# Linear attention: K and V read in 8 KB rows over eight heads, K's features kept twice, first matmul 128 wide

## Chip, cores and metric

The kernel runs on one core of a Trainium2 chip. The metric is device time in microseconds (us) of one execution. The core has these engines: PE (TensorE, matmuls; its weight loads are shown as PEld), DVE (VectorE), ACT (ScalarE), POOL (GpSimd) and SP (SyncE). DMAs are issued here by POOL and SP and run on 16 DMA engines that the queues share.

## The reference

```python
batch, heads, seq, dim = 8, 12, 512, 64          # Q, K, V: float32

Q_feat = np.maximum(0, Q) + 1
K_feat = np.maximum(0, K) + 1
KV = np.einsum('bhkd,bhkv->bhdv', K_feat, V)      # 64 x 64 per head
K_sum = np.sum(K_feat, axis=2)
numerator = np.einsum('bhqd,bhdv->bhqv', Q_feat, KV)
denominator = np.einsum('bhqd,bhd->bhq', Q_feat, K_sum)
return numerator / (denominator[:, :, :, None] + 1e-10)
```

There are 96 heads (batch times heads), each of 512 rows of 64 features. Three inputs of 12.58 MB are read and one output of 12.58 MB is written.

## The kernel before

**Tiling.** The 96 heads are handled as 12 groups of 8 heads, numbered 0 to 11, and the groups in 6 pairs (2s, 2s+1). The code calls the group `g` and the pair `s`. K and V are viewed with 16 sequence rows on a partition (`k_dram`, `v_dram`, C2 = 16), so one contiguous run in DRAM is 16 x 64 float32, 4 KB, and one 128-partition slab holds 4 heads, 32 partitions to a head. A group is two such slabs (index `n`, the slabs g and g + 2 of a pair's four). Q is viewed with 32 rows on a partition (`q_eights`), a run of 8 KB, 16 partitions to a head.

**Loads.** Except for the first K, which SP loads as float32 (`load_first_k`), all loads are issued by POOL and are turned from float32 into bf16 on the way. `load_pair(s)` issues K, V and Q of a pair, 2 MB each in DRAM and 1 MB in SBUF. `in_pool` has two buffers of each, so the loads of pair s + 2 are issued after the groups of pair s have used theirs; this stands at the end of an odd group's iteration.

**Per group.**
- `k_features(g)` (DVE, L137): kf = max(K + 1, 1), two instructions of 128 x 1024 elements.
- `v_blocks(g)`: V is copied into `v_all[:, g % 2]`, which is block-diagonal. Partitions 32b to 32b+31 (head b of a slab) have V in columns 64b to 64b+63, and ones in column 256 + b; the rest is zero. Three of the four copies are on DVE (L155), one is on ACT (L153).
- `keys_values(g)` (PE, L171): 32 matmuls with 64 columns of weights and a moving side of 260 columns. Slab n = 0 writes PSUM partitions 0 to 63, slab n = 1 writes 64 to 127. The two run side by side in two halves of the array. ACT then copies the result (`kva_ps`) into `kva_diag[g % 4]` in four instructions (L181, L182), again block-diagonal over n.
- `q_features`, `transposes` (PE L192 and ACT L195): the features of Q, transposed.
- `out_matmuls(g, h)` and `norms(g, h)` for h = 0, 1: 16 matmuls (L205) with `kva_diag` as the moving side, then a reciprocal (L222) and a product (L223) on DVE, twice. Here g is the pair member whose columns of Q are taken, and h chooses the K/V group: `kva_diag[(g // 2 * 2 + h) % 4]`. So h = 0 needs `keys_values` of the pair's even group and h = 1 that of its odd group.
- `store(g)`: 1 MB of output, by POOL for groups 0 to 9, by SP for 10 and (in two halves) 11.

**Order.** The order of instructions on every engine is the order written out in the code (`tc.manual_schedule()`). In the main loop (groups 0 to 9) an iteration of an odd group is: transposes(g-1), k_features(g), v_blocks(g), output(g-2), transposes(g), keys_values(g), loads and a store. An iteration of an even group is: k_features(g), v_blocks(g), output(g-2), q_features of g and g+1, keys_values(g), and a store. The last pair is written out by hand: k_features(10), output(8), out_matmuls(9, 0), v_blocks(10), k_features(11), v_blocks(11), keys_values(10), q_features of both, norms(9, 0), transposes(10), out_matmuls(9, 1), norms(9, 1), transposes(11), keys_values(11), output(10), output(11), stores. POOL's queue is in order too: a store that waits for its norms holds up the loads written behind it.

Of the kernel before, what the change touches and what calls it, by code (L numbers as in the profile page):

```python
# [8 lines left out]
FP32 = mybir.dt.float32  # L9
BF16 = mybir.dt.bfloat16  # L10
ALU = mybir.AluOpType
# [8 lines left out]
def kernel(  # L20
# [19 lines left out]
    nc = tc.nc  # L40

    B, H, S, D = Q.shape
    P = 128
    C = 8
    C2 = 2 * C
    C4 = 4 * C
    R = 4
    NPAIR = B * H * S // (P * C)
# [5 lines left out]
    def view(t, c):  # L54
        return t.flatten_outer_dims().rearrange("(n p c) d -> p n c d", p=P, c=c)

    q_eights = view(Q, C4)
    k_dram = view(K, C2)
    v_dram = view(V, C2)
    o_dram = view(out, C)  # L60

    const = ctx.enter_context(tc.tile_pool(name="const", bufs=1))
# [9 lines left out]
    psum_qt = ctx.enter_context(tc.tile_pool(name="psum_qt", bufs=2, space=bass.MemoryType.PSUM))  # L72

    identity = const.tile([P, P], BF16, name="identity")
    NV = 4
    v_all = const.tile([P, 2, 2, C2, 4 * D1], BF16, name="v_all")
    ones = const.tile([P, 4], BF16, name="ones")
    zero = const.tile([P, 1], FP32, name="zero")
    kva_all = const.tile([P, NV, 4, 2, D1], BF16, name="kva_all")
    kva_diag = [kva_all[:, i] for i in range(NV)]  # L80

    drams = dict(k=k_dram, v=v_dram)
    raw = {}
    bufs = {}
    kfs = {}
# [3 lines left out]
    cells_of = {}  # L89

    def load_first_k():
        k_raw = head_pool.tile([P, 2, C2, D], FP32, name="k_first")
        nc.sync.dma_start(out=k_raw, in_=k_dram[:, 0:4:2])
        raw["k", 0] = k_raw

    def load(x, groups):
        s = groups[0] // 2
        if groups[0] % 2 == 0 or (x, s) not in bufs:
            bufs[x, s] = in_pool.tile([P, 4, C2, D], BF16, name=f"{x}_raw")
        if len(groups) == 2:  # L100
            ms = slice(0, 4)
            of = slice(4 * s, 4 * s + 4)
        else:
            ms = slice(groups[0] % 2, 4, 2)
            of = slice(4 * s + groups[0] % 2, 4 * s + 4, 2)
        nc.gpsimd.dma_start(out=bufs[x, s][:, ms], in_=drams[x][:, of])  # L106
        for g in groups:
            raw[x, g] = bufs[x, s][:, g % 2 : 4 : 2]

    def load_q(s):  # L110
        t = in_pool.tile([P, 2, C4, D], BF16, name="q_raw")
# [28 lines left out]

    def k_features(g):
        k_raw = raw.pop(("k", g))
        kf = kf_pool.tile([P, C2, 2, D], BF16, name="kf")
        for n in range(2):
            feature(kf[:, :, n], k_raw[:, n])
        kfs[g] = kf

    def v_blocks(g):
        v_raw = raw.pop(("v", g))
        for b in range(4):  # L150
            ps = slice(32 * b, 32 * b + 32)
            if b == 3:
                nc.scalar.copy(out=v_all[ps, g % 2, :, :, b * D : b * D + D], in_=v_raw[ps])  # L153
            else:
                nc.vector.tensor_copy(  # L155
                    out=v_all[ps, g % 2, :, :, b * D : b * D + D], in_=v_raw[ps]
                )

    def q_features(g):
        q_raw = raw.pop(("q", g))  # L160
# [5 lines left out]
    def keys_values(g):  # L166
        kf = kfs.pop(g)
        kva_ps = psum_kva.tile([P, 4 * D1], FP32, name="kva_ps")
        for c in range(C2):
            for n in range(2):  # L170
                nc.tensor.matmul(  # L171
                    kva_ps[64 * n : 64 * n + 64],
                    lhsT=kf[:, c, n, :],
                    rhs=v_all[:, g % 2, n, c, :],
                    start=(c == 0),
                    stop=(c == C2 - 1),
                )
        kva = kva_diag[g % NV]
        for n in range(2):
            ps = slice(64 * n, 64 * n + 64)  # L180
            nc.scalar.copy(out=kva[ps, :, n, 0:D], in_=kva_ps[ps, 0 : 4 * D].rearrange("p (b d) -> p b d", b=4))  # L181
            nc.scalar.copy(out=kva[ps, :, n, D], in_=kva_ps[ps, 4 * D : 4 * D1])  # L182

    def transposes(g):
        qf = qfs.pop(g)
# [10 lines left out]

    def out_matmuls(g, h):
        qt = qts[g // 2]
        kva = kva_diag[(g // 2 * 2 + h) % NV]
        ops = [psum.tile([P, 2, BANK], FP32, tag="ps", name="o_ps") for _ in range(2)]  # L200
        for c in range(C):
            for j in range(2):
                b = 2 * (g % 2) + j
                q = 16 * (4 * h + b)
                nc.tensor.matmul(  # L205
                    ops[c // 4][64 * j : 64 * j + 64, c // 2 % 2, (c % 2) * W : (c % 2) * W + W],
                    lhsT=qt[:, c, q : q + 16, :],
                    rhs=kva[:, b],
                    start=True,
                    stop=True,  # L210
                )
        cells_of[g, h] = ops
# [19 lines left out]
    def output(g):  # L232
        for h in range(2):
            out_matmuls(g, h)
            norms(g, h)

    def clear(i):
        t = v_all[:, i].rearrange("p n c x -> p (n c x)").bitcast(FP32)
        w = t.shape[1] * 5 // 8
        nc.vector.memset(t[:, 0:w], 0.0)  # L240
        nc.scalar.copy(out=t[:, w:], in_=zero.to_broadcast([P, t.shape[1] - w]))  # L241
        nc.vector.tensor_copy(
            out=v_all[:, i, :, :, 4 * D : 4 * D1].rearrange("p n c j -> p (n c) j"),
            in_=ones[:, None, :].to_broadcast([P, 2 * C2, 4]),
        )

    with tc.manual_schedule():
        nc.gpsimd.memset(zero, 0.0)
        load_first_k()
        load("v", (0,))  # L250
        load_q(0)
        load("k", (1,))
        load("v", (1,))
        nc.vector.memset(ones, 0.0)
        for b in range(4):
            nc.vector.memset(ones[32 * b : 32 * b + 32, b : b + 1], 1.0)
        clear(0)
        make_identity(nc, identity)
        for t in kva_diag:
            for b in range(4):  # L260
                nc.gpsimd.memset(t[:, b], 0.0)  # L261
        load_pair(1)
        clear(1)
        last = NG - 1
        for g in range(last - 1):
            if g % 2:
                transposes(g - 1)
            k_features(g)
            v_blocks(g)
            if g >= 2:  # L270
                output(g - 2)
            if g % 2:
                transposes(g)
# [24 lines left out]
        output(last - 1)  # L298
        output(last)
        for g in range(last - LAG, NG):  # L300
            store(g)
# [30 lines left out]
```

## Time and profile before

| | us |
|---|---|
| time, median of 3 runs | 126.73 (126.72 to 127.41) |
| span of the profiled execution, first to last instruction | 125.0 |
| DVE busy in it | 89.1 (71%) |
| PE busy | 62.7 (50%) |
| ACT busy | 59.6 (48%) |
| POOL busy | 26.1 (21%) |
| read from and written to HBM | 37.75 MB and 12.58 MB, 403 GB/s over the span |

The page gives no separate whole time for the profiled execution; the median of the timed runs is 1.7 us above its span, and this is what lies before the first and after the last instruction. The page divides the span into 40 slices of 3.1 us, in which a digit is the busy share in tenths. The GB/s row counts bytes as written at the destination, so a stretch of loads that turn float32 into bf16 at 212 GB/s reads 424 GB/s from HBM. A group row has the count and shape of its instructions, their total busy time, the mean duration of one in ns, and the idle time of the engine ahead of them.

### The profile page before, as it was taken

How to read it: one execution, taken by the hardware profiler on the slowest of the kernel's cores; microseconds unless marked ns; L12 is line 12 of the kernel's file. 1: busy time of each engine (PE TensorE's matmuls, PEld its weight loads, DVE VectorE, ACT ScalarE, POOL GpSimd, SP SyncE). 2: the span in 40 equal slices, each digit the busy share in tenths (PEclk: the TensorE clock that was granted, in tenths of full speed). 3: DMA queues.
4: the chain of work that ended last, by engine and by line, in shares of the span. 5: the costliest groups of instructions: out<-in, count | busy, mean ns of one | idle time of the engine just before them, and what ended most of it. 6: DMA issues, size and time to landing. Idle time of an engine off the chain costs nothing.

```text
span 125.0 us, 2348 instructions
## 1 busy us (share of the span) xinstructions
PE 62.7 (50%) x960; PEld 51.3 (41%) x960; DVE 89.1 (71%) x190; ACT 59.6 (48%) x86; POOL 26.1 (21%) x52
## 2 busy tenths in 40 slices
PE   0004945200593837539684691079494457775300
PEld 0003735200482827428573491057393255663100
DVE  4895444206999899997999930799948699969700
ACT  7532289306029781956539462601992295450000
POOL 6991023000001630233302430302020200020000
PEclk9999999955589999995999679756999558997555
DMA  3999999999999999999999999999999999999992
GB/s 94 329 220 207 208 195 208 209 213 214 210 210 212 219 214 207 211 214 220 227 404 328 213 212 214 215 347 391 228 211 216 216 267 417 420 410 417 408 403 103
DMA packets 11803, 32.13 MB, mean 257 GB/s; under 512 B 528, under 2 KB 528, under 8 KB 11792
## 3 DMA queue, kind: packets, MB, share of 16 engines
q0 software_dynamic: 10448, 28.84, 97.2%
q1 hardware_dynamic: 1344, 3.15, 6.7%
q8 instruction: 7, 0.11, 0.3%
q14 instruction: 4, 0.03, 0.1%
HBM read 37.75 MB, written 12.58 MB: 403 GB/s over the span
## 4 chain that ended last, share of the span: by engine, by line
DMA 53%; DVE 23%; PE 8%; ACT 6%; issue 3%; POOL 2%; POOLq 0%
DMA v_raw<-in_V_dram 53%; DVE v_all L155 8%; DVE o_sb L223 8%; PE kva_ps L171 5%; ACT v_all L153 3%; DVE qf L137 2%; PE qt_ps L192 2%; DVE recip L222 2%; ACT qt L195 2%; DVE kf L137 1%; DVE qt L195 1%; ACT kva_all L181 1%; POOL v_raw L106 1%; POOL k_raw L106 1%; PE o_ps L205 1%
## 5 line engine op out<-in xcount | busy, mean ns | idle before, releaser
L205 PE MATMUL o_ps<-kva_all,qt 128*64 128x130 bf16 x384 | 20.5, 244 | 36.9 <-DVE recip L222 27.3
L171 PE MATMUL kva_ps<-v_all,kf 128*64 128x260 bf16 x384 | 30.1, 322 | 15.5 <-DVE v_all L155 15.3
L155 DVE COPY v_all<-v_raw 32x2048 bf16<-32x2048 bf16 x36 | 25.8, 717 | 13.5 <-DMA v_raw<-in_V_dram 13.1
L223 DVE TENSOR_TENSOR o_sb<-o_ps,recip 128x512 f32<-128x512 f32 x48 | 33.2, 692 | 1.7
L171 PEld LDWEIGHTS <-kf 128*64 128x64 bf16 x384 | 24.7, 131 | 18.8 <-DVE v_all L155 15.7
L205 PEld LDWEIGHTS <-qt 128*64 128x64 bf16 x384 | 14.3, 120 | 42.1 <-issue 27.3
L153 ACT COPY v_all<-v_raw 32x2048 bf16<-32x2048 bf16 x12 | 22.6, 1893 | 17.1 <-DMA v_raw<-in_V_dram 16.9
L195 ACT COPY qt<-qt_ps 128x1024 bf16<-128x1024 bf16 x23 | 22.2, 1015 | 6.7 <-PE qt_ps L192 6.4
L181 ACT CAST kva_all<-kva_ps 64x256 bf16<-64x256 f32 x24 | 8.9, 371 | 27.7 <-PE kva_ps L171 27.5
L126 POOL DMA_DIRECT2D out_dram<-o_sb x10 | 8.6, 863 | 35.9 <-DVE o_sb L223 27.5
L192 PE MATMUL qt_ps<-identity,qf 128*128 128x128 bf16 x192 | 14.9, 236 | 1.8 <-ACT qt L195 1.2
L192 PEld LDWEIGHTS <-qf 128*128 128x128 bf16 x192 | 12.5, 106 | 4.5 <-issue 2.5
L137 DVE TENSOR_SCALAR kf<-k_raw 128x1024 bf16<-128x1024 bf16 x22 | 8.5, 429 | 7.8 <-DMA k_raw<-in_K_dram 7.8
L106 POOL DMA_DIRECT2D k_raw<-in_K_dram x6 | 4.9, 811 | 35.2 <-DVE kf L137 35.2
L222 DVE RECIPROCAL recip<-o_ps 128x8 f32<-128x8 f32 x48 | 9.6, 200 | 1.4 <-PE o_ps L205 1.2
L137 DVE TENSOR_SCALAR qf<-q_raw 128x1024 bf16<-128x1024 bf16 x24 | 8.8, 432 | 2.1 <-DMA q_raw<-in_Q_dram 2.1
L106 POOL DMA_DIRECT2D v_raw<-in_V_dram x7 | 5.4, 766 | 13.1 <-ACT v_all L153 9.3
L240 DVE MEMSET v_all<- 128x2600 f32 x2 | 4.5, 2225 | 1.1 <-issue 1.1
L112 POOL DMA_DIRECT2D q_raw<-in_Q_dram x6 | 4.2, 708 | 0.0
L182 ACT CAST kva_all<-kva_ps 64x4 bf16<-64x4 f32 x24 | 4.1, 169 | 0.0
L241 ACT COPY v_all<-zero 128x1560 f32<-128x1560 f32 x2 | 2.9, 1488 | 0.0
L261 POOL MEMSET kva_all<- 128x130 bf16 x16 | 2.4, 201 | 0.0
(13 smaller groups left out, 5.7 us busy)
## 6 DMA issues: line engine op xcount, KB each, us to landing
out_dram<-o_sb POOLq DMA_DIRECT2D x10, 1024.0 KB, 25.9
q_raw<-in_Q_dram POOLq DMA_DIRECT2D x6, 1024.0 KB, 26.2
k_raw<-in_K_dram POOLq DMA_DIRECT2D x5, 1024.0 KB, 21.9
v_raw<-in_V_dram POOLq DMA_DIRECT2D x5, 1024.0 KB, 23.2
k_first<-in_K_dram SPq DMA_DIRECT2D x1, 1024.0 KB, 4.8
v_raw<-in_V_dram POOLq DMA_DIRECT2D x2, 512.0 KB, 10.7
out_dram<-o_sb SPq DMA_DIRECT2D x1, 1024.0 KB, 7.0
out_dram<-o_sb SPq DMA_DIRECT2D x2, 512.0 KB, 6.4
```

The costliest lines, as they stand in the source:

```text
L106: nc.gpsimd.dma_start(out=bufs[x, s][:, ms], in_=drams[x][:, of])
L126: nc.gpsimd.dma_start(out=o_to[:, g % 2 : 2 * NP : 2], in_=outs[s][:, g % 2 : 2 * NP : 2])
L137: nc.vector.tensor_scalar(out=dst, in0=src, scalar1=1.0, scalar2=1.0, op0=ALU.add, op1=ALU.max)
L153: nc.scalar.copy(out=v_all[ps, g % 2, :, :, b * D : b * D + D], in_=v_raw[ps])
L155: nc.vector.tensor_copy(out=v_all[ps, g % 2, :, :, b * D : b * D + D], in_=v_raw[ps])
L171: nc.tensor.matmul(kva_ps[64 * n : 64 * n + 64], lhsT=kf[:, c, n, :], rhs=v_all[:, g % 2, n, c, :], start=(c == 0), stop=(c == C2 - 1),)
L181: nc.scalar.copy(out=kva[ps, :, n, 0:D], in_=kva_ps[ps, 0 : 4 * D].rearrange("p (b d) -> p b d", b=4))
L192: nc.tensor.transpose(qt_ps[:, c, r], qf[:, r, 2 * half + c, :, :], identity)
L195: copy(out=qts[g // 2][:, lo : lo + 2], in_=qt_ps.rearrange("p c r q -> p c q r"))
L205: nc.tensor.matmul(ops[c // 4][64 * j : 64 * j + 64, c // 2 % 2, (c % 2) * W : (c % 2) * W + W], lhsT=qt[:, c, q : q + 16, :], rhs=kva[:, ...
L222: nc.vector.reciprocal(out=recip, in_=cells[:, :, :, :, D:D1])
L223: nc.vector.tensor_tensor(out=o_sb[:, 2 * h + g % 2 : 2 * NP : NP, 4 * i : 4 * i + 4].rearrange("p n (b c) d -> p b c n d", b=2), in0=cell ...
```

## The change

K and V are viewed as Q is: 32 rows on a partition, runs of 8 KB, 16 partitions to a head, 8 heads to a slab. A group is now one slab. The 32 partitions of a block of V now hold two heads (a = 0 and a = 1, 16 partitions each). So that one matmul does not mix the two, K's features are written twice, into two halves of 64 weight columns: copy a is max(K, 0) + 1 on the 16 partitions of head a of each block, and zero on the other head's. This is done with two per-partition scalars, `floor` and `shift` (0 and 1 on its own partitions, 3.4e38 and -3.4e38 on the others). The first matmul then has 128 columns of weights and writes all 128 PSUM partitions; the number of matmuls per group stays 32. `kva_all` is laid out by pair and by the pair's eight heads of a slab, and group g fills half n = g % 2 of it, so that `out_matmuls(g, h)` reads, for h = 0 and for h = 1, partitions that both groups of the pair have written. The number of instructions on ACT, PE and POOL stays; DVE gets 20 small memsets more at the start. The written order of the steps is unchanged.

```diff
-    k_dram = view(K, C2)
-    v_dram = view(V, C2)
+    k_eights = view(K, C4)
+    v_eights = view(V, C4)
...
     def k_features(g):
         k_raw = raw.pop(("k", g))
-        kf = kf_pool.tile([P, C2, 2, D], BF16, name="kf")
-        for n in range(2):
-            feature(kf[:, :, n], k_raw[:, n])
+        kf = kf_pool.tile([P, C4, 2, D], BF16, name="kf")
+        for a in range(2):
+            nc.vector.tensor_scalar(
+                out=kf[:, :, a],
+                in0=k_raw,
+                scalar1=floor[:, a : a + 1],
+                scalar2=shift[:, a : a + 1],
+                op0=ALU.max,
+                op1=ALU.add,
+            )
         kfs[g] = kf
...
     def keys_values(g):
         kf = kfs.pop(g)
         kva_ps = psum_kva.tile([P, 4 * D1], FP32, name="kva_ps")
-        for c in range(C2):
-            for n in range(2):
-                nc.tensor.matmul(
-                    kva_ps[64 * n : 64 * n + 64],
-                    lhsT=kf[:, c, n, :],
-                    rhs=v_all[:, g % 2, n, c, :],
-                    start=(c == 0),
-                    stop=(c == C2 - 1),
-                )
-        kva = kva_diag[g % NV]
-        for n in range(2):
-            ps = slice(64 * n, 64 * n + 64)
-            nc.scalar.copy(out=kva[ps, :, n, 0:D], in_=kva_ps[ps, 0 : 4 * D].rearrange("p (b d) -> p b d", b=4))
-            nc.scalar.copy(out=kva[ps, :, n, D], in_=kva_ps[ps, 4 * D : 4 * D1])
+        for c in range(C4):
+            nc.tensor.matmul(
+                kva_ps,
+                lhsT=kf[:, c],
+                rhs=v_all[:, g % 2, c, :],
+                start=(c == 0),
+                stop=(c == C4 - 1),
+            )
+        n = g % 2
+        kva = kva_all[64 * n : 64 * n + 64, g // 2 % NV]
+        for a in range(2):
+            ps = slice(64 * a, 64 * a + 64)
+            nc.scalar.copy(
+                out=kva[:, a:NE:2, n, 0:D], in_=kva_ps[ps, 0 : 4 * D].rearrange("p (b d) -> p b d", b=4)
+            )
+            nc.scalar.copy(out=kva[:, a:NE:2, n, D], in_=kva_ps[ps, 4 * D : 4 * D1])
...
     def out_matmuls(g, h):
         qt = qts[g // 2]
-        kva = kva_diag[(g // 2 * 2 + h) % NV]
+        kva = kva_all[:, g // 2 % NV]
...
-                    rhs=kva[:, b],
+                    rhs=kva[:, 4 * h + b],
...
+    def masks():
+        big = 3.4028234663852886e38
+        for a in range(2):
+            for t, own, other in ((floor, 0.0, big), (shift, 1.0, -big)):
+                first, rest = (other, own) if a else (own, other)
+                nc.vector.memset(t[:, a : a + 1], rest)
+                for b in range(4):
+                    nc.vector.memset(t[32 * b : 32 * b + 16, a : a + 1], first)
```

More of the change, by code (lines that the diff above doesn't have):

```diff
@@ L44 @@
     C = 8
-    C2 = 2 * C
     C4 = 4 * C
@@ L74 @@
     identity = const.tile([P, P], BF16, name="identity")
-    NV = 4
-    v_all = const.tile([P, 2, 2, C2, 4 * D1], BF16, name="v_all")
+    NV = 2
+    NE = 8
+    v_all = const.tile([P, 2, C4, 4 * D1], BF16, name="v_all")
     ones = const.tile([P, 4], BF16, name="ones")
     zero = const.tile([P, 1], FP32, name="zero")
-    kva_all = const.tile([P, NV, 4, 2, D1], BF16, name="kva_all")
-    kva_diag = [kva_all[:, i] for i in range(NV)]
-    drams = dict(k=k_dram, v=v_dram)
+    floor = const.tile([P, 2], FP32, name="floor")
+    shift = const.tile([P, 2], FP32, name="shift")
+    kva_all = const.tile([P, NV, NE, 2, D1], BF16, name="kva_all")
+    drams = dict(k=k_eights, v=v_eights)
     raw = {}
@@ L91, in load_first_k @@
     def load_first_k():
-        k_raw = head_pool.tile([P, 2, C2, D], FP32, name="k_first")
-        nc.sync.dma_start(out=k_raw, in_=k_dram[:, 0:4:2])
+        k_raw = head_pool.tile([P, C4, D], FP32, name="k_first")
+        nc.sync.dma_start(out=k_raw, in_=k_eights[:, 0])
         raw["k", 0] = k_raw
@@ L98, in load @@
         if groups[0] % 2 == 0 or (x, s) not in bufs:
[L99 to L105, printed above, removed]
+            bufs[x, s] = in_pool.tile([P, 2, C4, D], BF16, name=f"{x}_raw")
+        ms = slice(groups[0] % 2, groups[-1] % 2 + 1)
+        of = slice(groups[0], groups[-1] + 1)
         nc.gpsimd.dma_start(out=bufs[x, s][:, ms], in_=drams[x][:, of])
         for g in groups:
-            raw[x, g] = bufs[x, s][:, g % 2 : 4 : 2]
+            raw[x, g] = bufs[x, s][:, g % 2]
     def load_q(s):
@@ L151, in v_blocks @@
             ps = slice(32 * b, 32 * b + 32)
[L152 to L156, printed above, removed]
-                )
+            copy = nc.scalar.copy if b == 3 else nc.vector.tensor_copy
+            copy(out=v_all[ps, g % 2, :, b * D : b * D + D], in_=v_raw[ps])
     def q_features(g):
@@ L168, in keys_values @@
         kva_ps = psum_kva.tile([P, 4 * D1], FP32, name="kva_ps")
-        for c in range(C2):
-            for n in range(2):
-                nc.tensor.matmul(
-                    kva_ps[64 * n : 64 * n + 64],
-                    lhsT=kf[:, c, n, :],
-                    rhs=v_all[:, g % 2, n, c, :],
-                    start=(c == 0),
-                    stop=(c == C2 - 1),
-                )
-        kva = kva_diag[g % NV]
-        for n in range(2):
-            ps = slice(64 * n, 64 * n + 64)
-            nc.scalar.copy(out=kva[ps, :, n, 0:D], in_=kva_ps[ps, 0 : 4 * D].rearrange("p (b d) -> p b d", b=4))
-            nc.scalar.copy(out=kva[ps, :, n, D], in_=kva_ps[ps, 4 * D : 4 * D1])
+        for c in range(C4):
[14 more added lines that the diff above has]
+            nc.scalar.copy(out=kva[:, a:NE:2, n, D], in_=kva_ps[ps, 4 * D : 4 * D1])
     def transposes(g):
@@ L235, in output @@
             norms(g, h)
+    def masks():
[6 more added lines that the diff above has]
+                    nc.vector.memset(t[32 * b : 32 * b + 16, a : a + 1], first)
     def clear(i):
-        t = v_all[:, i].rearrange("p n c x -> p (n c x)").bitcast(FP32)
+        t = v_all[:, i].rearrange("p c x -> p (c x)").bitcast(FP32)
         w = t.shape[1] * 5 // 8
@@ L242, in clear @@
         nc.vector.tensor_copy(
-            out=v_all[:, i, :, :, 4 * D : 4 * D1].rearrange("p n c j -> p (n c) j"),
-            in_=ones[:, None, :].to_broadcast([P, 2 * C2, 4]),
+            out=v_all[:, i, :, 4 * D : 4 * D1],
+            in_=ones[:, None, :].to_broadcast([P, C4, 4]),
         )
@@ L256 @@
             nc.vector.memset(ones[32 * b : 32 * b + 32, b : b + 1], 1.0)
+        masks()
         clear(0)
         make_identity(nc, identity)
-        for t in kva_diag:
-            for b in range(4):
-                nc.gpsimd.memset(t[:, b], 0.0)
+        for v in range(NV):
+            for i in range(NE):
+                nc.gpsimd.memset(kva_all[:, v, i], 0.0)
         load_pair(1)
```

## The prediction

> **What bounds the kernel now.** I read the slices first, then the groups, then windows of the DMA, then the end of the timeline.
>
> ```profile
> DVE  4895444206999899997999930799948699969700
> PEclk9999999955589999995999679756999558997555
> DMA  3999999999999999999999999999999999999992
> GB/s 94 329 220 207 208 195 208 209 213 214 210 210 212 219 214 207 211 214 220 227 404 328 213 212 214 215 347 391 228 211 216 216 267 417 420 410 417 408 403 103
> ```
>
> The DMA engines are full from the second slice to the last but one: 50.3 MB pass at 403 GB/s. No engine is full all the time (DVE 89.1 of 125.0 us). So the transfers bound the kernel, and the chain of waits, which gives 53% to V's DMA, shows a transfer standing in the queue behind others. The question is where an engine comes so late that the queue runs dry. A transfer of the middle has time to spare: by the page's DMA issues a load lands 22 to 26 us (medians) after its issue, while its 1 MB in SBUF takes 5 us at 212 GB/s; the rest it stands in the queue. The end has less:
>
> ```profile
> 88.00:97.00 9.00, 5.46 (x112) 4.48 (x106) 6.85 (x18) 6.44 (x9) 0.75 (x1) 1.00 1.12 215
> 78.00:82.00 4.00, 0.00 (x0) 0.03 (x1) 3.16 (x6) 1.89 (x1) 1.13 (x1) 0.75 1.05 216
> 116.00:118.00 2.00, 0.69 (x10) 0.40 (x8) 1.80 (x5) 0.00 (x0) 0.00 (x0) 0.50 1.01 408
> 118.00:120.00 2.00, 0.00 (x0) 0.00 (x0) 0.00 (x0) 0.00 (x0) 0.00 (x0) 0.50 1.05 409
> 122.00:123.00 1.00, 0.00 (x0) 0.00 (x0) 0.00 (x0) 0.00 (x0) 0.00 (x0) 0.50 0.61 238
> 93.75 0.62 PE L205 MATMUL o_ps<-kva_all,qt 128*64 128x130 bf16 x16
> 94.75 0.20 DVE L222 RECIPROCAL recip<-o_ps 128x8 f32<-128x8 f32 x1
> 99.10 2.08 DVE L155 COPY v_all<-v_raw 32x2048 bf16<-32x2048 bf16 x3 [0.90 <-DMA v_raw<-in_V_dram]
> 108.81 1.98 PE L171 MATMUL kva_ps<-v_all,kf 128*64 128x260 bf16 x32
> 110.62 0.62 PE L205 MATMUL o_ps<-kva_all,qt 128*64 128x130 bf16 x16
> 111.06 0.21 DVE L222 RECIPROCAL recip<-o_ps 128x8 f32<-128x8 f32 x1 [1.16 <-PE o_ps L205]
> 114.54 0.38 SPq L129 DMA_DIRECT2D out_dram<-o_sb  x1
> 116.22 2.05 SPq L132 DMA_DIRECT2D out_dram<-o_sb  x2
> ```
>
> In the window rows the last column is GB/s and the one ahead of it the DMA share; the others are a timeline. The last V lands at 99.1; DVE, then PE with keys_values(11), then DVE again lead to the first norm of group 10 at 111.06, and eight norms later the last store is issued at 117.9. The DMA meanwhile drains stores at 408 GB/s, 2.57 us for 1 MB, until about 122.6 (238 of 408 in the last window). Counting back from there, the two halves of store 11 start at 121.3 and 120.0 and store 10 at 117.5. Store 10 is issued at 114.54; SP's first load was issued at 0.74 and moved from about 2.2 (94 GB/s in a slice of 3.1 us, against 329 in the next, are its last 0.9 us), so a store needs about 1.4 us from issue to its first packet and it could have moved from about 115.95. **The end therefore tolerates 1.55 us of delay in group 10's norms; what is later shifts the end one for one.**
>
> **The parts.**
>
> ```profile
> L171 PE MATMUL kva_ps<-v_all,kf 128*64 128x260 bf16 x384 | 30.1, 322 | 15.5 <-DVE v_all L155 15.3
> L155 DVE COPY v_all<-v_raw 32x2048 bf16<-32x2048 bf16 x36 | 25.8, 717 | 13.5 <-DMA v_raw<-in_V_dram 13.1
> L137 DVE TENSOR_SCALAR kf<-k_raw 128x1024 bf16<-128x1024 bf16 x22 | 8.5, 429 | 7.8 <-DMA k_raw<-in_K_dram 7.8
> L181 ACT CAST kva_all<-kva_ps 64x256 bf16<-64x256 f32 x24 | 8.9, 371 | 27.7 <-PE kva_ps L171 27.5
> L182 ACT CAST kva_all<-kva_ps 64x4 bf16<-64x4 f32 x24 | 4.1, 169 | 0.0
> ```
>
> *Rows of 8 KB.* Five windows of nothing but K and V (4 KB runs) move 207 to 215 GB/s, mean 212; five of nothing but Q (8 KB runs) 214 to 221, mean 216. K and V by POOL are 12.06 MB in SBUF, so 56.9 us become 55.8: 1.1 us won, all of it before the last V lands. From below, nothing; from above, the best Q window against the mean K/V one, 2.4 us. The Trainium skill's page "DMA: Bandwidth & Descriptors" (section Specifications) asks only for 512 bytes or more for full rate, so by it both row sizes run alike and this term is zero; the windows above show 2%.
>
> *K's features.* Two instructions of 128 x 2048 instead of 128 x 1024, with scalars from SBUF. By shape: 1024 elements take 422 ns (median), the 2048 of L155 684, so 0.26 ns per element and 0.16 us fixed; then one costs 0.69 and a group 0.5 to 0.6 us more, 6.5 us over 12 groups. Whether an instruction with scalars per partition keeps that rate no row shows. The other bound is L223, 512 elements in 692 ns, 1.04 ns per element: 2.29 us for one, 3.7 more per group. I take 0.69, because operation, types and memory are those of the L137 row. The Trainium skill's "Vector Engine (DVE) Microarchitecture Reference" (section 5.1, Performance modes) names only source and destination as conditions of the fast modes, which would give 0.69 too; no run here shows it yet.
>
> *First matmul.* At full clock the 32 starts of a group take 1.98 us to the end: 110 ns for a pair of 260 columns that run side by side. A 128-wide one fills the array, so 32 take 32 x 0.11 = 3.5 us plus 0.2, **3.7 instead of 2.0**. (The 128-wide transposes start every 56 ns for 128 columns, so wide weight loads are hidden.) At half clock a group now takes 3.7 and would take 7.
>
> *A new wait.* out_matmuls(g, 0) of an even g read what keys_values(g) had left long before. Now they need the four ACT copies of keys_values(g+1), which stands just ahead of them on PE: 0.9 us (0.37 + 0.17, twice, partly overlapped), plus 0.3 to the first norm. Behind the waiting matmul stand the pair's other output matmuls, and DVE's norms wait for them.
>
> *Start.* 20 memsets at 0.09 us (the four of `ones` took 0.35) are 1.8 us, and the first float32 K takes about 1.2 more; DVE idles some 13 us before the V of group 2 is handled at 29.2, and that cover takes both. Fewer descriptors in POOL's issues are worth 0.05 us each, hidden.
>
> **The sum along the path.** In an odd group's iteration PE begins the transposes about 1.3 us before DVE's norms end (56.0 against 57.3 in group 5), and they take 1.1. Then come keys_values and the next group's first output, 0.25. Up to now that is -1.3 + 1.1 + 2.0 + 0.25 = 2.05 us after the norms' end, and DVE has features and V blocks for 0.77 + 2.1 = 2.9: no wait. With the change PE is ready at -1.3 + 1.1 + 3.7 + 0.9 + 0.3 = 4.7, DVE at 1.4 + 2.1 = 3.5: a wait of 1.2 us per pair, beside 1.1 us more of features, 2.3 in all.
>
> From 43.9 to 72.3 DVE has next to no idle time, so this piles up over two pairs: 4.6, less the 0.8 that DVE waits for V at 58, is 3.8. Norms(5) end at 76.1 instead of 72.3. DVE's wait for V(8), 4.2 us until 78.7 (now about 77.8), swallows it: keys_values(7) is done at 79.6, its copies at 80.5, norms(6) start at 80.8 (80.9 before). After that there is no such cover. Norms(7) end 0.5 later by the features of group 9, at 92.7 (92.2 before); transposes(9) 91.4 to 92.5, keys_values(9) to 96.2, copies to 97.1, norms(8) 97.4 to 100.9 instead of 94.75 to 98.2. V of group 10 has landed at 98.0, DVE takes it at 100.9 instead of 99.1: **1.8 us late**.
>
> From there to norms(10) it was 11.96 us (99.1 to 111.06). Now come on top: k_features(11) 0.6, keys_values(11) 1.7, its copies and the first output 1.0: **3.3 us**. If keys_values(10) runs at half clock, as the stretch from 97 to 104 does now, some 0.5 more: I take 3.6. Norms(10) are 1.8 + 3.6 = 5.4 us late, less 1.55 tolerated: **3.85 us**. The profiled span becomes 125.0 + 3.85 = 128.85; with the 1.7 us that lie around it, and so against the median of 126.73, **130.6 us**. The gain from the rows hardly counts in it, since V no longer sets when DVE goes on.
>
> **Rivals.**
> - *The queue hides it all.* For it: the DMA row is full throughout, and in the middle the queue is long. Against: the three terms of keys_values(11) alone exceed 1.55. If they cost under 1.55 together, the time is 126.7 - 1.1 = 125.6, not slower.
> - *Only the last pair is hit.* If norms(8) are not held up, DVE takes V(10) at 98.0, 1.1 early: 3.3 - 1.1 - 1.55 = 0.65 us, 127.4. Against: the first output after keys_values(9) runs at 93.75 now, 1.0 us before norms(8), and 1.7 + 0.9 are to be added.
> - *Scalars from SBUF lose the packed rate.* At half (1.22 us each) another 1.1 per group, twice or three times on the path: 133.5. At one element per cycle DVE has 18 x 1.86 = 33.5 us more after 29.2, where 74.7 remain now: 29.2 + 108.2 + 7.1 from the last norm to the end + 1.7 = 146.
> - *The clock.* With keys_values(9) and (10) both at half clock, 3 us more: 133.8. In the forecast's upper part.
>
> **Chances.** Forecast (tail 2 to 7 us late net) 0.72, its own range 128.4 to 134; all hidden 0.07; only the last pair 0.08; slow features 0.13. The time is the forecast's. The range goes down to 127.6 and up to 135, leaving out the first two rivals and the slowest features. A difference of 1% is about what a measurement of this kernel can tell from none: faster by more 0.04, within 0.11, slower 0.85.
>
> **What would show it.** Right: L171 at 384 matmuls, 128 wide, 3.5 to 3.8 us a group at full clock; kf near 690 ns; a DVE wait of recip for PE o_ps ahead of each even group's norms; K/V windows near 216 GB/s; a last V that lands about 1 us earlier; and a DMA row with a gap between 112 and 122 us. Wrong: kf rows of 1.2 us or more; stores that stay back to back to the end; norms(8) that end before the last V lands.

## The result, and the profile after

| | before | after |
|---|---|---|
| time, median of 6 runs each (us) | 127.03 (126.36 to 127.47) | 135.05 (133.90 to 135.63) |
| ratio, with its 95% interval | | 1.0616 (1.0568 to 1.0664) |
| profiled execution: time, span (us) | span 125.0 | 135.63, 133.9 |

The change costs 8.0 us between the medians, where 3.85 were forecast; the time forecast was 130.6 us. Ratios, here and below, leave out executions that ran in a slower state of the chip; the medians are of all. The profiled execution of after is the upper end of its six; its span is 8.9 us longer than the span before, and the readings below explain those 8.9.

The slices of the page of after (names and order as before):

```profile
DVE  4899961266999929989599898799922999933960
PEclk9999999689996897799977999999869856999955
DMA  4999999999999999999999999999999999216095
GB/s 120 308 214 212 213 214 214 215 215 213 214 215 214 215 215 214 212 214 315 389 228 214 215 214 323 382 231 214 213 212 279 416 421 414 121 61 257 23 381 222
```

The DMA row was full to its last slice but one; it now has a hole of four slices (121, 61, 257, 23 GB/s), 113.8 to 127.2 us. The prediction had named a gap between 112 and 122 us as a sign of being right. Bytes that could have moved there had not been computed yet. The chain of waits says the same. Its summary lines on the page of after:

```profile
PE 42%; DVE 35%; ACT 15%; issue 4%; ACTq 0%; DVEq 0%
PE kva_ps L170 35%; DVE o_sb L225 14%; DVE v_all L157 6%; ACT qt L197 5%; ACT v_all L157 4%; ACT kva_all L181 4%; DVE kf L142 4%; PE o_ps L207 3%; DVE v_all L251 3%; DVE recip L224 3%; PE qt_ps L194 3%; DVE qf L134 2%; ACT kva_all L184 1%; DVE v_all L253 1%; DVE shift L246 0%
```

Before, V's transfer held 53% of that chain and the first matmul 5%. Now no transfer is in it at all, and the first matmul alone holds 35%. **The kernel was bound by its transfers and is now bound by its engines.** The groups of the changed lines (busy time, mean ns of one, idle time ahead):

```profile
L170 PE MATMUL kva_ps<-v_all,kf 128*128 128x260 bf16 x384 | 55.4, 312 | 17.6 <-DVE v_all L157 15.6
L157 DVE COPY v_all<-v_raw 32x2048 bf16<-32x2048 bf16 x36 | 26.3, 730 | 4.6 <-DMA v_raw<-in_V_dram 4.2
L142 DVE TENSOR_SCALAR kf<-k_raw,floor,shift 128x2048 bf16<-128x2048 bf16 x22 | 17.2, 824 | 3.0 <-DMA k_raw<-in_K_dram 2.9
L224 DVE RECIPROCAL recip<-o_ps 128x8 f32<-128x8 f32 x48 | 9.6, 200 | 16.6 <-PE o_ps L207 16.5
```

The matmul's busy time rises from 30.1 to 55.4 us, the features' from 8.5 to 17.2. DVE's idle time has changed hands: ahead of V's copies it waited 13.1 us for V's transfers and now 4.2, ahead of the reciprocals it now waits 16.5 us for PE. The view of DVE's waits (us in total, times, longest) makes it eight waits, of at most 4.9 us; before there was one such wait, of 1.2:

```profile
DVE recip L224 <- PE o_ps L207: 16.5, 8, 4.9
DVE v_all L157 <- DMA v_raw<-in_V_dram: 4.2, 2, 3.3
```

Where the waits stand, in the timeline of after (start, duration; in brackets how long the engine was idle and for whom):

```profile
42.01 1.89 PE L194 MATMUL qt_ps<-identity,qf 128*128 128x128 bf16 x16
43.69 4.27 PE L170 MATMUL kva_ps<-v_all,kf 128*128 128x260 bf16 x32
49.40 0.21 DVE L224 RECIPROCAL recip<-o_ps 128x8 f32<-128x8 f32 x1 [2.72 <-PE o_ps L207]
58.26 0.21 DVE L224 RECIPROCAL recip<-o_ps 128x8 f32<-128x8 f32 x1 [0.43 <-PE o_ps L207]
61.83 3.74 PE L170 MATMUL kva_ps<-v_all,kf 128*128 128x260 bf16 x32 [0.32 <-ACT v_all L157]
65.60 0.37 ACT L181 CAST kva_all<-kva_ps 64x256 bf16<-64x256 f32 x1 [1.87 <-PE kva_ps L170]
66.98 0.21 DVE L224 RECIPROCAL recip<-o_ps 128x8 f32<-128x8 f32 x1 [1.36 <-PE o_ps L207]
75.70 0.21 DVE L224 RECIPROCAL recip<-o_ps 128x8 f32<-128x8 f32 x1 [0.30 <-PE o_ps L207]
84.43 0.21 DVE L224 RECIPROCAL recip<-o_ps 128x8 f32<-128x8 f32 x1 [1.36 <-PE o_ps L207]
96.08 5.35 PE L170 MATMUL kva_ps<-v_all,kf 128*128 128x260 bf16 x32
102.84 0.21 DVE L224 RECIPROCAL recip<-o_ps 128x8 f32<-128x8 f32 x1 [4.90 <-PE o_ps L207]
117.38 3.74 PE L170 MATMUL kva_ps<-v_all,kf 128*128 128x260 bf16 x32
122.54 0.21 DVE L224 RECIPROCAL recip<-o_ps 128x8 f32<-128x8 f32 x1 [4.16 <-PE o_ps L207]
126.02 0.39 SPq L126 DMA_DIRECT2D out_dram<-o_sb  x1
```

The reciprocals shown are the first of groups 2, 3, 4, 5, 6, 8 and 10. Each of an even group follows an odd group's keys_values on PE, its copies on ACT and the first output matmul: 65.60, where the copies start, to 66.98 is 1.38 us. The starts of the five even groups before were 46.1, 61.1, 80.9, 94.8 and 111.1, so their norms are late by 3.3, 5.9, 3.5, 8.0 and 11.5 us. The 11.5 of group 10, less what the end tolerates, are the 8.9.

In numbers per pair: K, V and Q of a pair are 3.15 MB in SBUF, 14.8 us at 212 GB/s, and its stores 2 x 2.57 = 5.1 us, 19.9 together. The engines of after need 17.5 (66.98 to 84.43), of which DVE is busy 15.5. That is less than 19.9, and yet it sets the end: the loads come first at 14.8 us per pair, the last V lands at 98.5 and the last Q at 104.4 (the trace's landing records), and after that only stores are left, each waiting for its norms. Before, the engines kept up with the loads (46.1 to 61.1 is one pair in 15.0), and the stores of the last groups stood ready.

### The profile page after: what moved, and what is told of

It reads as the page before. It is cut to its first block, busy times and chain, and to the rows that moved or that the text cites. A ratio compares the mean times of both kernels' runs of the same rounds, so it can differ in the third digit from the quotient of the medians.

```text
span 133.9 us, 2361 instructions
## 1 busy us (share of the span) xinstructions
PE 87.1 (65%) x960; PEld 67.6 (50%) x960; DVE 100.5 (75%) x210; ACT 59.6 (45%) x86; POOL 25.2 (19%) x52
## 3 DMA queue, kind: packets, MB, share of 16 engines
q1 hardware_dynamic: 1216, 3.15, 6.4%
## 4 chain that ended last, share of the span: by engine, by line
PE 42%; DVE 35%; ACT 15%; issue 4%; ACTq 0%; DVEq 0%
PE kva_ps L170 35%; DVE o_sb L225 14%; DVE v_all L157 6%; ACT qt L197 5%; ACT v_all L157 4%; ACT kva_all L181 4%; DVE kf L142 4%; PE o_ps L207 3%; DVE v_all L251 3%; DVE recip L224 3%; PE qt_ps L194 3%; DVE qf L134 2%; ACT kva_all L184 1%; DVE v_all L253 1%; DVE shift L246 0%
## 5 line engine op out<-in xcount | busy, mean ns | idle before, releaser
L170 PE MATMUL kva_ps<-v_all,kf 128*128 128x260 bf16 x384 | 55.4, 312 | 17.6 <-DVE v_all L157 15.6
L170 PEld LDWEIGHTS <-kf 128*128 128x128 bf16 x384 | 42.1, 111 | 29.1 <-DVE v_all L157 15.8
L157 DVE COPY v_all<-v_raw 32x2048 bf16<-32x2048 bf16 x36 | 26.3, 730 | 4.6 <-DMA v_raw<-in_V_dram 4.2
L207 PEld LDWEIGHTS <-qt 128*64 128x64 bf16 x384 | 13.7, 114 | 28.5 <-DVE o_sb L225 16.0
L224 DVE RECIPROCAL recip<-o_ps 128x8 f32<-128x8 f32 x48 | 9.6, 200 | 16.6 <-PE o_ps L207 16.5
L142 DVE TENSOR_SCALAR kf<-k_raw,floor,shift 128x2048 bf16<-128x2048 bf16 x22 | 17.2, 824 | 3.0 <-DMA k_raw<-in_K_dram 2.9
L194 PE MATMUL qt_ps<-identity,qf 128*128 128x128 bf16 x192 | 13.8, 227 | 2.0 <-ACT qt L197 2.0
L103 POOL DMA_DIRECT2D k_raw<-in_K_dram x6 | 4.1, 692 | 38.2 <-DVE kf L142 38.2
L103 POOL DMA_DIRECT2D v_raw<-in_V_dram x7 | 4.8, 692 | 21.6 <-ACT v_all L157 14.6
L142 DVE TENSOR_SCALAR kf<-k_first,floor,shift 128x2048 bf16<-128x2048 f32 x2 | 2.6, 1342 | 0.0
## 6 DMA issues: line engine op xcount, KB each, us to landing
k_raw<-in_K_dram POOLq DMA_DIRECT2D x5, 1024.0 KB, 17.6
```

The source lines that it names most:

```text
L142: nc.vector.tensor_scalar(out=kf[:, :, a], in0=k_raw, scalar1=floor[:, a : a + 1], scalar2=shift[:, a : a + 1], op0=ALU.max, op1=ALU.add,)
L157: copy(out=v_all[ps, g % 2, :, b * D : b * D + D], in_=v_raw[ps])
L170: nc.tensor.matmul(kva_ps, lhsT=kf[:, c], rhs=v_all[:, g % 2, c, :], start=(c == 0), stop=(c == C4 - 1),)
L194: nc.tensor.transpose(qt_ps[:, c, r], qf[:, r, 2 * half + c, :, :], identity)
L207: nc.tensor.matmul(ops[c // 4][64 * j : 64 * j + 64, c // 2 % 2, (c % 2) * W : (c % 2) * W + W], lhsT=qt[:, c, q : q + 16, :], rhs=kva[:, ...
L224: nc.vector.reciprocal(out=recip, in_=cells[:, :, :, :, D:D1])
```

## The experiments

The theory under test is the prediction's: the wide matmul and the new wait, with the copies, hold up DVE's norms once per pair, and the delay is handed on. The rivals lay the time on DVE's doubled features, or on the clock. "Added" below is the ratio less 1, times the median of before on the same chip. On that scale after adds 7.8 us (7.2 to 8.4).

### Each part alone, added to before

**rows_only**: K and V loaded in 8 KB rows, all else as before.

```diff
-    k_dram = view(K, C2)
-    v_dram = view(V, C2)
+    k_eights = view(K, C4)
+    v_eights = view(V, C4)
...
-            raw[x, g] = bufs[x, s][:, g % 2 : 4 : 2]
+            raw[x, g] = bufs[x, s][:, g % 2].rearrange("p (n c) d -> p n c d", n=2)
...
```

> The kernel before with nothing changed but the loads: K and V in rows of 8 KB (the first K too), all else as before. The rows of a partition then belong to other heads than the arithmetic assumes, so this run is for its time alone. Theory A (the rows move 1 to 2% faster and everything else in the change costs time): 126.0 to 126.7 us against 127.0 of before, K/V windows at 214 to 216 GB/s instead of 212. Rival (row size does not matter from 4 KB on): within 0.2 us of before.

Measured: 126.25 us, ratio 0.9947 (0.9927 to 0.9967), added -0.7 us. A window of its K and V loads (last two columns DMA share and GB/s):

```profile
48.00:56.50 8.50, 5.08 (x95) 4.31 (x90) 8.27 (x20) 5.01 (x8) 2.40 (x4) 0.98 1.07 215
```

215 GB/s against the 212 of the 4 KB rows. The rows do win about what was computed, but a gain of half a per cent is all that they hold.

**before_features**: the doubled instruction alone (scalars 0 and 1 from SBUF everywhere, so each copy is the whole feature).

```diff
-        kf = kf_pool.tile([P, C2, 2, D], BF16, name="kf")
-        for n in range(2):
-            feature(kf[:, :, n], k_raw[:, n])
+        kf = kf_pool.tile([P, 2, 2, C2, D], BF16, name="kf")
+        for a in range(2):
+            nc.vector.tensor_scalar(
+                out=kf[:, a],
+                in0=k_raw,
+                scalar1=floor[:, 0:1],
+                scalar2=shift[:, 0:1],
+                op0=ALU.max,
+                op1=ALU.add,
+            )
...
-                    lhsT=kf[:, c, n, :],
+                    lhsT=kf[:, n, n, c, :],
...
```

> The kernel before with the doubled feature instructions alone: each K feature instruction has 128 x 2048 elements and two scalars per partition (0 and 1 everywhere), half of the result is used, the output is unchanged. Theory A: 0.7 us more of DVE per group, inside DVE's waits for V in the middle, 0.7 us later norms of the last pair, inside the tolerance of the end: 126.7 to 127.5 us. Rival B: 129 us or more.

Measured: 126.92 us, ratio 1.0007 (0.9992 to 1.0023), added 0.1. Its group:

```profile
L147 DVE TENSOR_SCALAR kf<-k_raw,floor,shift 128x2048 bf16<-128x2048 bf16 x22 | 17.6, 842 | 4.8 <-DMA k_raw<-in_K_dram 4.7
```

Some 9 us of DVE time more (17.6 against 8.5) cost nothing, because DVE waited for transfers in before.

**before_wide**: 128 columns of weights in the first matmul, nothing else.

```diff
-                    kva_ps[64 * n : 64 * n + 64],
-                    lhsT=kf[:, c, n, :],
+                    kva_ps,
+                    lhsT=kf[:, c],
...
-                    start=(c == 0),
-                    stop=(c == C2 - 1),
+                    start=(c == 0 and n == 0),
+                    stop=(c == C2 - 1 and n == 1),
```

> The kernel before with the wide matmul alone: each of the 32 first matmuls of a group takes both slabs' K features as 128 columns of weights, so that the sums mix what should be separate; loads, features, copies and their waits stay. Theory A (wide matmul, wait and features each nearly fit in the slack of before and are dear only together): 127.0 to 129 us. Rival (the wide matmul alone is the cost, as the loss of 6.6 us in after_narrow may suggest): 132 us or more.

**before_wait**: the outputs of both halves read what the pair's odd group wrote, so that h = 0 waits too.

```diff
-        kva = kva_diag[(g // 2 * 2 + h) % NV]
+        kva = kva_diag[(g // 2 * 2 + 1) % NV]
```

> The kernel before with the wait alone: both h of the output matmuls read the K/V product of the pair's odd group, so that the first output matmul behind keys_values of that group waits for its copies on ACT; the even group's product is left unused. Theory A: 0.9 us more in the loop, inside DVE's slack in the middle and inside the tolerance of the end: 126.7 to 127.5 us, no change. Rival C (the wait is a main cost by itself): 129 us or more.

**before_wide_wait**: both of these edits.

> Both of these in the kernel before: the wide matmul (sums mixed) and the wait for the odd group's copies. Features single, rows 4 KB. Theory A: the two add on PE's way from one norm to the next, 129 to 131.5 us, more than the sum of the two alone. Rival: the sum of the two single runs.

Measured: before_wide 128.65 us, ratio 1.0131 (1.0068 to 1.0194), added 1.7; before_wait 126.86, ratio 1.0021 (1.0002 to 1.0039), added 0.3; before_wide_wait 131.87, ratio 1.0394 (1.0337 to 1.0451), added 5.0 (4.3 to 5.7), a little above the 129 to 131.5 us expected. **The two together cost 3.0 us more than one and the other.** In before_wide_wait, with the old rows and the old features, DVE again waits eight times for PE, 15.8 us against 16.5 in after. Not all eight stand ahead of the same groups; the four longest do (ahead of norms(2), (4), (8) and (10): 2.60, 2.48, 3.66 and 4.15 us):

```profile
DVE recip L222 <- PE o_ps L205: 15.8, 8, 4.2
```

### Each part taken out of after

**after_narrow**: 64 columns of weights again, the two halves of the array used in turn.

```diff
-                kva_ps,
-                lhsT=kf[:, c],
+                kva_ps[64 * (c % 2) : 64 * (c % 2) + 64],
+                lhsT=kf[:, c, c % 2, :],
...
-                start=(c == 0),
-                stop=(c == C4 - 1),
+                start=(c < 2),
+                stop=(c >= C4 - 2),
```

> The changed kernel, but each of its 32 first matmuls of a group loads only 64 of the 128 weight columns and writes one half of PSUM, turn and turn about, so two run side by side as before; sums over half of the rows are left out. Loads, doubled features, layout of kva_all and its wait stay. Theory A (the wide matmul is the long link in a loop of PE, ACT and DVE that each pair of groups goes round): L170 back to 2.0 us a group at full clock, and 127 to 128.5 us instead of 135. Rival B (DVE with its doubled features sets the pace): 133 or more. Rival C (the wait for the copies): 131 or more.

**after_no_wait**: the outputs read a slot that no group of the pair writes.

```diff
-    NV = 2
+    NV = 3
...
-        kva = kva_all[:, g // 2 % NV]
+        kva = kva_all[:, (g // 2 + 2) % NV]
...
```

> The changed kernel, but the output matmuls of a pair read the kva_all slot of the pair before (three slots instead of two), so that no output matmul waits for the four copies that follow keys_values just ahead of it on PE. Matmul widths, features and loads stay; the output uses another pair's K and V. Theory A: about 1 us less per pair over five pairs, 130 to 132.5 us. Rival C (this wait is the main cost): 128.5 or less. Rival B: no change, 134 to 135.5.

**after_narrow_no_wait**: both edits.

> The changed kernel with 64-wide first matmuls (sums over half of the rows left out) and with the output matmuls on another pair's slot, no wait for the copies: what is left of the change are the rows, the doubled features and the memsets. Theory A: DVE's 0.7 us per group remain, 8.4 us a group against 7.5 that the transfers need, 126.5 to 128 us.

**after_one_feature**: one features instruction per group; the second half of the weights is a constant.

```diff
-        kf = kf_pool.tile([P, C4, 2, D], BF16, name="kf")
-        for a in range(2):
+        kf = kf_all[:, g % 2]
+        for a in range(1):
...
```

> The changed kernel with only the first of the two K feature instructions of a group; the second half of the weights is a constant set once at the start by POOL. The other head's features are left out. DVE loses some 9 us of work. Theory A (DVE has slack in the loop): 133.5 to 135 us. Rival B (DVE's doubled features set the pace): 128 to 130 us.

Measured: after_narrow 128.45 us, ratio 1.0101 (1.0056 to 1.0147); after_no_wait 129.46, ratio 1.0211 (1.0171 to 1.0251), a little below what the theory expected; after_narrow_no_wait 126.70, ratio 0.9984 (0.9968 to 0.9999); after_one_feature 132.67, ratio 1.0455 (1.0431 to 1.0478), a little below the theory's 133.5 to 135 and far above the 128 to 130 of the rival that lays the time on DVE's features. DVE's waits for PE in after_narrow, and then in after_one_feature:

```profile
DVE recip L224 <- PE o_ps L207: 7.8, 5, 2.8
```

```profile
DVE recip L225 <- PE o_ps L208: 21.1, 9, 4.2
```

Without the second features instruction DVE merely waits longer for PE, 21.1 us instead of 16.5. With narrow matmuls that wait is halved. Before, after and these seven runs in one table, added us:

| | neither | wait | wide | wide and wait |
|---|---|---|---|---|
| 4 KB rows, old features | 0 | 0.3 | 1.7 | 5.0 |
| 8 KB rows, both feature copies | -0.2 | 1.3 | 2.7 | 7.8 |
| 8 KB rows, one feature copy | | | | 5.8 |

Down the columns the rest of the change (rows, the second feature copy, the new layout and the memsets) costs 1 to 2.8 us wherever wide or wait is there, and nothing without them: after_narrow_no_wait, which keeps all of that, takes as long as before. The 1.0 in the column "wide" is at the edge of its noise. Along a row, wide and wait together cost more than their sum. Taking out the wide matmul brings back 6.5 us, the wait 5.1, a feature copy 2.0: 13.6 in all, of the 7.8 that there are. This fits one loop with several links, in which shortening any one helps only until another bound takes over.

### Where along the kernel it is lost

**after_pair1_free**, **after_early_free**, **after_late_free**: as after_no_wait, but only pair 1, only pairs 0 to 3, or only pairs 4 and 5 are freed of the wait. What the freed pairs read in its place is a third slot, of ones.

```diff
-        kva = kva_all[:, g // 2 % NV]
+        kva = kva_all[:, 2 if g // 2 == 1 else g // 2 % 2]
...
```

(The condition is `< 4` in after_early_free and `> 3` in after_late_free.)

> The changed kernel in which the output matmuls of groups 2 and 3 alone read a constant third slot of kva_all, so that the first output matmul behind keys_values(3) waits for no copies; all other pairs wait as in the change; the K/V product of that pair is left unused. In the changed kernel the norms of group 2 start at 49.4 us instead of 46.1, the first place where it falls behind, and the forecast had no delay there. Theory A (from there on the loop is slower than the transfers, so that what is lost early is never regained): norms(2) about 1 us earlier and about 1 us off the time, 133.8 to 134.4 us. Rival (the later pairs set the end whatever comes before): no change, 135 us.

> The changed kernel in which the output matmuls of groups 0 to 7 (pairs 0 to 3) read a constant third slot of kva_all and so wait for no copies; those of groups 8 to 11 wait as in the change; the K/V products of pairs 0 to 3 are left unused. The forecast had DVE's wait for V of group 8 swallow everything that piles up before it, so by the forecast this changes nothing: 135 us. Theory A (the pile-up starts a pair earlier than the forecast had it, is larger than that wait, and passes on to the end): norms(6) start near 81 to 82 us instead of 84.4, and 131.5 to 133.5 us.

> The same for groups 8 to 11 alone (pairs 4 and 5): their output matmuls read the constant slot and wait for no copies, those of pairs 0 to 3 wait as in the change. By the forecast all of the wait's cost that counts is here, two waits of 0.9 us: 133 to 133.5 us. Theory A: about the same two waits, 132.5 to 133.5 us, so that this and the run with the early pairs freed together make up the 5.6 us that freeing all pairs took away.

Measured: pair 1 alone 134.47 us, ratio 1.0557 (1.0518 to 1.0596), added 7.1, not to be told from after: inconclusive as a time. Pairs 0 to 3: 131.79 us, ratio 1.0354 (1.0287 to 1.0420), added 4.5. Pairs 4 and 5: 133.06 us, ratio 1.0482 (1.0438 to 1.0526), added 6.1. The prediction had the early pairs' delay swallowed; freeing them wins 3.3 us and freeing the late ones 1.7 (each give or take 1), together about the 5.1 that freeing all wins. **So a delay of the first pairs does reach the end.** In the timeline of after_early_free, V's copies of group 8, group 10's first norm and the first store that SP issues:

```profile
78.76 2.17 DVE L157 COPY v_all<-v_raw 32x2048 bf16<-32x2048 bf16 x3 [0.87 <-DMA v_raw<-in_V_dram]
117.72 0.21 DVE L224 RECIPROCAL recip<-o_ps 128x8 f32<-128x8 f32 x1 [3.98 <-PE o_ps L207]
121.20 0.39 SPq L126 DMA_DIRECT2D out_dram<-o_sb  x1
```

The last two are 4.8 us earlier than in after, though the wait ahead of the norm is nearly the same (3.98 against 4.16). Of the 4.8, 3.5 are there at norms(6), which start at 80.97 instead of 84.43, about as expected; the rest comes with keys_values(9), which ran at full clock in this execution (3.74 instead of 5.35 us). So did keys_values(3) and the transposes ahead of it, so the 3.5 are not the wait's alone: what the edit and what the clock gave there is not told apart. The first line shows the other side of it: here norms(5) end at 76.2, so DVE is ready before V(8) has landed, waits 0.87 us for it, and what is left of the delay is swallowed as the prediction had it.

In after_pair1_free the norms of group 2 start at 46.87 instead of 49.40, those of groups 4 and 6 2.1 earlier, those of group 10 at 120.0 instead of 122.5. So most of the 2.5 us is handed on from pair to pair. Not all of it is the wait's: in that execution the transposes ahead of keys_values(3) and keys_values(3) itself also ran at full clock (1.07 and 3.74 us instead of 1.89 and 4.27), and the later bursts ran at other clocks than in after.

### The clock

**after_warm**: five matmuls of filler on the identity behind each output tile, from group 2 on, into columns of PSUM that nobody reads. **after_warm7**: 25 of them in output(7) only, just ahead of keys_values(9).

```diff
+            if c % 4 == 3 and 2 <= g:
+                for _ in range(5):
+                    nc.tensor.matmul(
+                        ops[c // 4][:, 0, 320:448], lhsT=identity, rhs=identity, start=True, stop=True
+                    )
```

```diff
+            if g == 7 and c == 4 * (1 - h) + 3:
+                for _ in range(20 if h == 0 else 5):
+                    nc.tensor.matmul(
+                        ops[c // 4][:, 0, 320:448], lhsT=identity, rhs=identity, start=True, stop=True
+                    )
```

> The changed kernel with five more matmuls (identity by identity, into PSUM columns that nothing reads) behind each output tile from group 2 on, 0.28 us each time, so that PE is busy while DVE's norms pace it; the output is unchanged. In the changed kernel seven of the twelve first-matmul bursts run partly at half clock, 4.3 to 5.9 us instead of 3.75. Theory A with the clock (those bursts stand in the loop): bursts from group 4 on at 3.8 us and 130 to 132.5 us. Rival (the clock only fills time that PE would wait for DVE): 134 us or more.

> The changed kernel with 25 more matmuls (identity by identity, into columns that nothing reads) between the output matmuls of group 7, where PE waits for DVE, so that the clock should still be full when keys_values(9) begins; the output is unchanged. Theory A with the clock: that burst 3.75 us instead of 5.35, norms(8) 1.6 us earlier, 133.4 to 134.2 us. Rival (no slow burst is on the path): 135 us.

Measured: after_warm 134.66 us, ratio 1.0645 (1.0585 to 1.0705), added 8.2: no gain. Its clock and DMA rows:

```profile
PEclk9999999599996899999999999999999999999995
DMA  4999999999999999999999999999999999525095
```

The clock was granted nearly throughout (mean 0.96 against 0.88), every keys_values from group 4 on took 3.74 or 3.75 us, and the expected 130 to 132.5 still failed to come; the hole in the DMA row is still there. Group 8's norms start at 101.8, only 1.0 earlier than in after. One reason can be read: at full clock an even group's keys_values lies beside 8.5 us of DVE work and was never on the path. Another is that the fillers cost time themselves: they write into the tile that DVE waits for, and the line that its waits name there is L216, that of the fillers, so five of them (0.28 us) stand in each such wait. How much the clock alone would bring over the whole kernel is not settled by this run.

after_warm7 puts fillers in one place: 133.47 us, ratio 1.0531 (1.0502 to 1.0560), added 6.7, as the theory expected. Its timeline at group 9:

```profile
95.21 3.74 PE L170 MATMUL kva_ps<-v_all,kf 128*128 128x260 bf16 x32
100.37 0.21 DVE L229 RECIPROCAL recip<-o_ps 128x8 f32<-128x8 f32 x1 [3.09 <-PE o_ps L207]
```

keys_values(9) takes 3.74 us instead of 5.35, the wait behind it 3.09 instead of 4.90, and the time falls by 1.1 us (about 0.4 to 1.8). Norms(8) start 2.5 us earlier than in after; 0.8 of that is there at norms(6) already, ahead of the fillers, and 1.6 is what the burst is shorter. So the half clock in that one burst did cost time, and the 1.6 us that it was longer lie within what was measured.

## Why the prediction fell short

*Rows of 8 KB.* Right in size: the loads of after move 212 to 215 GB/s in most slices and 217 in a window of the middle (87.5 to 96.5; forecast 216), and alone the rows win 0.7 us (forecast 1.1, with bounds 0 and 2.4). Right too that they hardly count in the sum, since V no longer sets when DVE goes on (its waits for V fell from 13.1 to 4.2 us).

*K's features.* 0.82 us instead of 0.69 on the page, 1.52 to 1.66 us for the two of a group in the timeline of after; the rate stayed packed, so the rival of the scalars from SBUF fell. The small miss is 0.14 to 0.28 us per group.

*First matmul.* 3.74 us per group at full clock: as forecast (3.7). The wide matmul gives up the two halves of the array that worked side by side. The Trainium skill's "TensorEngine Tiling (Array Packing)", section Theoretical Speedup, gives up to 2x where the small dimension is at most 64, and after_narrow shows what that is worth here: a burst of 32 at full clock takes 1.96 us instead of 3.74, and the kernel 6.5 us less.

*A new wait.* Forecast 1.2 us from the end of keys_values to the norm, measured 1.38. As a mechanism right: the reciprocals ahead of every even group's norms now wait for PE.

*A period of a pair.* The 14.9 us before (46.1 to 61.1) and the 2.3 us forecast for a pair make 17.2; measured 17.45 (66.98 to 84.43). Right, for a pair whose odd group runs at full clock.

*How large the early delay is, and what V(8)'s wait can swallow.* **This is the step that failed**: "this piles up over two pairs: 4.6, less the 0.8 that DVE waits for V at 58, is 3.8", and then "DVE's wait for V(8), 4.2 us until 78.7 (now about 77.8), swallows it". The stretch from 43.9 on holds the waits ahead of norms(2) and norms(4), which the sum takes at 1.2 us each, and so it has norms(5) end at 76.1. They ended at about 79.1 (they start at 75.7), 3.0 later. Half of that is the wait ahead of norms(2): 2.72 us instead of 1.2, since the transposes ahead of keys_values(3) and that burst itself ran in part at half clock, 1.89 and 4.27 us instead of 1.07 and 3.74. Ahead of norms(3) and norms(5), where the sum has no wait, DVE waited 0.43 and 0.30 us, behind keys_values(4) and (6), which took 5.39 and 5.04. And V(4)'s copies began at 44.41, already 0.5 us late.

So the delay was 6.8 us where 3.8 were forecast. The end of norms(5) lies past the 77.8 (measured 78.5) at which V(8) lands, so DVE had no wait left, and norms(6) start at 84.43, 3.6 us later than the forecast 80.8: the 3.0, and 0.6 more on PE's way, of which 0.32 is a wait for ACT's copy of V. after_early_free shows that this counts: with the early waits gone (and the early odd bursts at full clock in its profile) norms(5) end at 76.2, DVE waits for V(8) again, and 3.3 us come back. The mechanism of the swallowing was right; the delay that it was to swallow was taken too small.

That the clock made the wait ahead of norms(2) longer shows in after_warm7, whose matmuls are the same up to group 7 and which had that stretch at full clock:

```profile
41.18 1.07 PE L194 MATMUL qt_ps<-identity,qf 128*128 128x128 bf16 x16
42.63 3.74 PE L170 MATMUL kva_ps<-v_all,kf 128*128 128x260 bf16 x32 [0.38 <-ACT v_all L157]
47.82 0.21 DVE L229 RECIPROCAL recip<-o_ps 128x8 f32<-128x8 f32 x1 [1.40 <-PE o_ps L207]
```

The wait is 1.40 us there. (In that execution the half clock fell on keys_values(7) instead, 5.39 us, with 2.71 us of wait ahead of norms(6), which start at 83.60, late as well.) The profile of before had a warning: in group 5, from which the sum takes its 1.3 us, the transposes that it counts at 1.1 and the burst that it counts at 2.0 ran at

```profile
56.03 1.88 PE L192 MATMUL qt_ps<-identity,qf 128*128 128x128 bf16 x16
57.84 2.76 PE L171 MATMUL kva_ps<-v_all,kf 128*64 128x260 bf16 x32
```

Before, DVE waited for V just then and nothing showed. The text of after_pair1_free says that the forecast had no delay at group 2; by the sum one of its two waits of 1.2 us stands there.

*The clock at the end.* keys_values(9) was taken at 3.7 us and ran 5.35, its first 3.3 us at half clock; norms(8), forecast for 97.4, start at 102.84, 5.4 late against the forecast's own time, 1.8 more than the 3.6 before. after_warm7 gives that back (1.1 us between the ratios, 2.3 between the spans of the profiled executions, 133.9 and 131.6). keys_values(10) took 5.89 us where 3.7 and some 0.5 were allowed for, and norms(10) stand 6.1 us behind the forecast. The rival named "The clock" came nearest, at 133.8: its mechanism is there, and what it lacks is the same half clock in the early pairs.

*The tolerance at the end.* Forecast 1.55 us, measured 2.6: norms(10) are 11.5 us late and the span 8.9 longer. From the last issue of a store to the end it took 7.1 us before (117.9 to 125.0) and takes 4.5 now (129.4 to 133.9), because the queue is empty when the stores come. This miss went the other way.

So, in the terms of the sum: 5.4 us late were forecast and 11.5 measured; 3.6 of the difference are at norms(6), from the early delay that was too large to be swallowed, 1.8 from keys_values(9) and 0.7 from keys_values(10) and what lies about it. The rivals "the queue hides it all" and "only the last pair is hit" are refuted by the hole in the DMA row and by group 2's wait. What stays open: how the early 3.0 us divide in other executions, and what the time would be at full clock throughout. The six executions of after spread over 1.7 us, and the ones with less granted clock are the longer (0.893 at 133.9, 0.874 at 135.63), but 0.883 stands at 134.8 and 0.884 at 135.63; which bursts run at half clock differs from one execution to the next, so the share of each burst is that of the profiled one only.

## What to carry to other kernels

An edit that saves half a per cent of a full queue can still lose six if it lengthens a loop between engines: write down the loop that each stage goes round (here PE, ACT, PE, DVE), its period, and the pace of the transfers that it must follow, and look at parts together, since two that cost 0.3 and 1.7 us alone cost 5.0 together. A stall absorbs a delay once, up to its own length, so add the delay up stage by stage, with each term as long as the rows of that very stage show it (here at half clock too), and compare it with the stall before crossing it out. A stretch in which the loads set the pace and the stores are left for the end has less slack than its full DMA row shows.

## What the runs showed of the hardware

Half clock after a stretch of half work. Windows of after around keys_values(9), and two from 10 us earlier (columns: us, busy time and count of PE, PEld, DVE, ACT and POOL, granted clock, DMA share, GB/s):

```profile
82.32:85.73 3.41, 1.84 (x31) 1.27 (x28) 1.98 (x5) 2.63 (x5) 0.26 (x1) 1.00 1.02 411
85.73:89.14 3.41, 2.99 (x35) 2.47 (x32) 3.34 (x9) 0.14 (x1) 0.75 (x1) 1.00 1.06 265
92.56:95.97 3.41, 1.61 (x31) 1.35 (x32) 3.24 (x9) 2.76 (x3) 0.00 (x0) 1.00 1.06 214
95.97:99.38 3.41, 3.41 (x21) 2.40 (x18) 1.97 (x3) 1.74 (x2) 0.75 (x1) 0.50 1.08 217
99.38:102.80 3.42, 2.65 (x33) 2.13 (x32) 0.00 (x0) 1.29 (x5) 0.00 (x0) 1.00 1.00 223
```

A PE that was busy for 1.61 of 3.41 us was granted 0.50 of its clock for the next 3.41 us, though it was busy all through them, and all of it afterwards. Cut into windows of this length and phase, the profile of after shows the same from 14 us on: the eight windows with PE busy for 1.7 us or less are each followed by half clock, those with 1.84 or more by full clock. So the border lies near half in this execution; in others it is less sharp (in before a window with 1.97 us is followed by half clock, one with 1.69 by full). The Trainium skill's "TensorE: Matmul & The Clock Gate" (Part 1, What's actually happening) gives 3.4 us windows and the half clock after an idle one; the length agrees, while the window ahead of this drop was not idle. With 25 fillers in that place the drop did not come.

A feature instruction with two scalars per partition took 824 ns in the mean (842 in before_features), against 730 for a copy of 2048 elements on a quarter of the partitions: dearer than the copy by an eighth, and far from the 2.29 us that the prediction had as its other bound. Rows of 8 KB instead of 4 KB are worth 1 to 2% of a loading rate of 212 GB/s.
